# Masked softmax over 16 batches: stores in whole 16 KB packets, each held until the load five batches on has landed

## The chip, the core and the metric

The kernel runs on one core of a Trainium2 chip. The metric is the device time of the whole program in microseconds, as a median of several runs; the profile is a further execution, recorded by the hardware. The core's compute engines work beside 16 DMA engines, which move data between the chip's main memory (DRAM below) and the on-chip memory in which the tile `xt` lies.

## The reference: what is computed

The input `x` has 16 batches of 8 heads x 256 queries x 256 keys in float32: 2,048 rows of 256 numbers, 2 MB, for each batch. A vector `lengths` gives each batch the number of keys that count. Each row is a softmax over its first `length` keys, and zero behind them.

```python
for b in range(batch):
    length = lengths[b]
    masked = x[b, :, :, :length].copy()
    masked = masked - np.max(masked, axis=-1, keepdims=True)
    exp_masked = np.exp(masked)
    result[b, :, :, :length] = exp_masked / np.sum(exp_masked, axis=-1, keepdims=True)
```

The lengths of this draw are 188, 233, 229, 243, 195, 252, 165, 210, 222, 180, 209, 157, 159, 199, 214 and 248. The kernel does without the row's maximum.

## The kernel before: the parts that matter

A batch lies on 128 partitions, 16 rows of 256 numbers on each, so that one partition's share is 16 KB in one piece, in DRAM and in `xt` alike. `xt` has eight slots; batch b sits in slot b modulo 8 from its load to the end of its store.

**Loads.** The first four batches come whole, issued by the SP queue. Batches 4 to 15 are issued by GpSimd (POOL), which reads the length and loads only so many columns as are needed, in steps of eight (160, 168, ... 240, and 256 for the two longest): 16 short rows per partition rather than one long piece. Load n waits until load n-2 has landed and until store n-8, the last user of the slot, has landed.

```python
slots = 8
ahead = 4
...
for h in range(2):
    s = slice(h * half, (h + 1) * half)
    nc.sync.dma_start(out=xt[:, 0, s], in_=x_f[0, :, s]).then_inc(s_ld[h], 16)
for b in range(1, ahead):
    nc.sync.dma_start(out=xt[:, b], in_=x_f[b]).then_inc(s_ld[b + 1], 16)
...
nc.gpsimd.wait_ge(s_ld[ahead - 1], 16)
with nc.Fori(0, (batch - ahead) // 2, 1, engines=[POOL]) as q:
    for par in range(2):
        n = 2 * q + (ahead + par)
        v_len = length(POOL, word[0:1, bass.ds(2 * n, 1)])
        with nc.gpsimd.If(q >= 1):
            nc.gpsimd.wait_ge(s_sw[par], 16 * q)
            nc.gpsimd.wait_ge(s_st[par], 64 * q)
        pick(v_len, bass.ds(n, 1), bass.ds(n % slots, 1), par, widths + [seq_k])
...
# in pick, for the width w found:
nc.gpsimd.dma_start(out=xt[:, slot, :, :w], in_=x_n[:, n, :, :w]).then_inc(s_sw[par], 16)
```

`s_ld[3]` is the semaphore of batch 2. The semaphores `s_st` start at 64, set by GpSimd.

**Stores.** The SP queue stores a batch in parts. The first batch and batch 13 go whole, batches 1 to 7 as a half and two quarters, the rest in two halves. A half is 8 KB per partition, a quarter 4 KB. A part waits until its rows are divided (`s_out`); the first part of batch b also waits until store b-2 has landed.

```python
def parts(b):
    if b == 0:
        cuts = [0, nt]
    elif b < 8:
        cuts = [0, half, half + quarter, nt]
    elif b != batch - 3:
        cuts = [0, half, nt]
    else:
        cuts = [0, nt]
    return [slice(i, j) for i, j in zip(cuts, cuts[1:])]
...
nc.sync.wait_ge(s_exp, 3)
for b in range(batch):
    s_b = s_st[b % 2]
    for s in parts(b):
        nc.sync.wait_ge(s_out, 2 * b + (s.stop - 1) // half + 1)
        if b >= 2 and s.start == 0:
            nc.sync.wait_ge(s_b, 64 * (b // 2 + 1))
        nc.sync.dma_start(
            out=out_f[b, :, s, :], in_=xt[:, b % slots, s, :]
        ).then_inc(s_b, 16 * ((s.stop - s.start) // quarter))
```

**Compute.** Per batch VectorE (DVE) pushes the columns behind the length to a very negative number (`clip` in `mask`, one pass), ScalarE (ACT) takes 16 exponentials with their row sums, and DVE takes the reciprocals and multiplies, in two halves. Batch 4's mask waits for load 4, and so on.

Of the kernel before, what the change touches and what calls it, by code (L numbers as in the profile page):

```python
# [20 lines left out]
def kernel(  # L21
# [6 lines left out]
    nc = tc.nc  # L28
    P = nc.NUM_PARTITIONS

    batch, heads, seq_q, seq_k = x.shape
    rows = heads * seq_q
    assert rows % P == 0
    nt = rows // P
    half = nt // 2
    quarter = nt // 4
# [3 lines left out]

    slots = 8
    ahead = 4
    assert slots - ahead == 4 and batch % slots == 0

    widths = list(range(160, 248, 8))
    low = widths[0]
# [2 lines left out]

    def parts(b):  # L50


        if b == 0:
            cuts = [0, nt]
        elif b < 8:
            cuts = [0, half, half + quarter, nt]
        elif b != batch - 3:
            cuts = [0, half, nt]
        else:
            cuts = [0, nt]  # L60
        return [slice(i, j) for i, j in zip(cuts, cuts[1:])]

    pool = ctx.enter_context(tc.tile_pool(name="all", bufs=1))
# [17 lines left out]
    with tc.tile_critical(no_gpsimd_drain=True):  # L81
# [6 lines left out]
        s_sw = [sem("s_sw0"), sem("s_sw1")]  # L88
# [5 lines left out]
        s_exp = sem("s_exp")  # L94
# [15 lines left out]
        for b in range(1, ahead):  # L110
            nc.sync.dma_start(out=xt[:, b], in_=x_f[b]).then_inc(s_ld[b + 1], 16)  # L111

        nc.sync.wait_ge(s_exp, 3)
        for b in range(batch):
            s_b = s_st[b % 2]
            for s in parts(b):
                nc.sync.wait_ge(s_out, 2 * b + (s.stop - 1) // half + 1)
                if b >= 2 and s.start == 0:
# [4 lines that stand above are left out]
# [167 lines left out]
```

The softmax here doesn't subtract the row's maximum and nothing guards it: scores larger than these inputs give would overflow.

## Time and profile before

| | before |
|---|---|
| median of 3 runs | 156.5 us (156.17 to 156.55) |
| span of the profiled execution | 154.3 us |
| bytes moved by DMA | 62.08 MB: 28.51 MB read from DRAM, 33.55 MB written to it |
| mean rate over the span | 402 GB/s |
| DVE busy | 115.4 us (75%) |
| ACT busy | 105.2 us (68%) |
| POOL busy | 19.0 us (12%) |

In the page, a span is cut into 40 equal slices, and a digit is the busy share of a slice in tenths. A DMA queue (q0, q1) is a stream of transfers; q1 is that of SP, q0 that of GpSimd. A transfer is cut into packets, each of which one of the 16 DMA engines moves in one go. The records of the single packets in the trace give queue, start, duration and size of each; where the text speaks of packets' durations it means these. A window's line gives start and end, length, busy time of each engine with the number of its instructions, the granted clock, the DMA engines' mean busy share and the rate.

### The profile page before, as it was taken

The page shows a single profiled execution, that of the slowest core. Times are in us where ns is not written, and L with a number is a line of the kernel's source. Part 1 is how long each engine was busy: PE and PEld are TensorE (multiplying, and loading weights), DVE is VectorE, ACT ScalarE, POOL GpSimd, SP SyncE. Part 2 cuts the span into 40 slices and gives each one's busy share as a digit, 9 for nine tenths or more (in the row PEclk, how much of TensorE's full clock was granted, in tenths as well). Part 3 has the DMA queues.
Part 4 walks back from the last instruction along what each step waited for, and adds up shares of the span by engine and source line. Part 5 has one row for each costly group of instructions (what it writes and reads, how often), then busy time and mean ns, then how long its engine had stood idle before and what let it go on. Part 6 is the DMA issues. An engine that isn't in the chain of part 4 may idle for free.

```text
span 154.3 us, 1325 instructions
## 1 busy us (share of the span) xinstructions
PE 0.2 (0%) x1; PEld 0.1 (0%) x1; DVE 115.4 (75%) x84; ACT 105.2 (68%) x514; POOL 19.0 (12%) x25
## 2 busy tenths in 40 slices
PE   0000000000000000000000000000000000000000
PEld 0000000000000000000000000000000000000000
DVE  1339999952999696988969696969698692599500
ACT  3097799992592969779595959596877907988000
POOL 4910031000320200202011020202010000000000
DMA  4999999999999999999999999999999999999993
GB/s 117 427 450 420 437 365 409 400 408 452 407 406 390 415 404 417 412 413 415 405 419 413 414 412 405 416 416 420 417 416 423 418 431 435 418 444 418 423 431 130
DMA packets 10132, 62.08 MB, mean 402 GB/s; under 512 B 866, under 2 KB 962, under 8 KB 6290
## 3 DMA queue, kind: packets, MB, share of 16 engines
q1 hardware_dynamic: 6048, 41.95, 66.0%
q0 software_dynamic: 4080, 20.12, 32.2%
q14 instruction: 2, 0.02, 0.0%
q10 hardware_dynamic: 2, 0.00, 0.0%
HBM read 28.51 MB, written 33.55 MB: 402 GB/s over the span
## 4 chain that ended last, share of the span: by engine, by line
DMA 54%; DVE 25%; issue 7%; ACT 5%; ACTq 2%; SPq 1%; POOLq 1%; DVEq 0%
DMA xt<-in_x_dram 33%; DMA out_dram<-xt 21%; DVE xt L222 14%; DVE xt L195 9%; ACT xt L251 5%; ACTq L251 1%; DVE inv_sum L219 1%; SPq L109 1%; POOLq L99 0%; SPq L120 0%; SPq L111 0%; DVEq L212 0%; POOLq L130 0%; POOLq L135 0%; ACTq L246 0%
## 5 line engine op out<-in xcount | busy, mean ns | idle before, releaser
L251 ACT ACTIVATE xt<-xt x256 | 102.3, 401 | 35.2 <-DVE xt L195 35.2
L222 DVE TENSOR_TENSOR xt<-xt,inv_sum 128x2048 f32<-128x2048 f32 x32 | 73.4, 2292 | 1.1
L195 DVE SCALAR_TENSOR_TENSOR xt<-down,len_s,xt 128x2048 f32<-128x2048 f32 (+1 forms) x17 | 37.8, 2221 | 14.1 <-DMA xt<-in_x_dram 14.0
L251 ACT ACTIVATION_READ_ACCUMULATOR xt<-xt x256 | 47.9, 187 | 0.0
L130 POOL DMA_DIRECT2D xt<-in_x_dram x12 | 12.8, 1064 | 94.6 <-issue 48.7
L219 DVE RECIPROCAL inv_sum<-row_sum 128x8 f32<-128x8 f32 x32 | 6.3, 198 | 12.1 <-ACT xt L251 12.1
L149 POOL MEMSET xt<- 128x1536 f32 x4 | 5.3, 1386 | 1.1 <-DVE len_s L186 1.1
L243 ACT ACT_TABLE_LOAD x1 | 1.3, 1283 | 1.6 <-SPq L81 1.6
L178 DVE TENSOR_SCALAR down<-iota_i 128x256 f32<-128x256 int32 x1 | 0.3, 297 | 1.6 <-POOL iota_i L141 1.6
L183 DVE CAST len_b<-word 1x16 bf16<-1x16 int32 x1 | 0.2, 164 | 0.4 <-DMA word<-in_lengths_dram 0.4
L186 DVE TENSOR_SCALAR len_s<-len_f 128x16 f32<-128x16 f32 x1 | 0.2, 174 | 0.4 <-PE len_f L165 0.4
L141 POOL IOTA iota_i<- 128x256 int32 x1 | 0.3, 332 | 0.6 <-SPq L81 0.6
L146 POOL MEMSET seed<- 1x1 f32 x2 | 0.3, 162 | 0.0
L243 ACT ACTIVATE warm<-const-float32-0.0 128x1 f32<-128x1 f32 x1 | 0.2, 203 | 0.0
L144 POOL MEMSET ones<- 1x128 bf16 x1 | 0.2, 194 | 0.0
L165 PE MATMUL len_f<-len_b,ones 1*128 1x16 bf16 x1 | 0.2, 168 | 2.6 <-DVE len_b L183 2.6
L274 POOL MEMSET const-float32-0.0<- 128x1 f32 x1 | 0.1, 98 | 0.3 <-issue 0.3
L165 PEld LDWEIGHTS len_f<-len_b,ones 1*128 1x128 bf16 x1 | 0.1, 97 | 2.6 <-POOL ones L144 2.6
L274 POOL MEMSET const-float32-1.0<- 128x1 f32 x1 | 0.1, 98 | 0.0
L274 POOL MEMSET const-bfloat16-1.0<- 128x1 bf16 x1 | 0.1, 98 | 0.0
L274 POOL MEMSET const-uint8-127<- 128x1 uint8 x1 | 0.1, 98 | 0.0
L274 POOL BASE_LOAD x1 | 0.0, 17 | 0.1
## 6 DMA issues: line engine op xcount, KB each, us to landing
out_dram<-xt SPq DMA_DIRECT2D x21, 1024.0 KB
out_dram<-xt SPq DMA_DIRECT2D x14, 512.0 KB
xt<-in_x_dram SPq DMA_DIRECT2D x3, 2048.0 KB, 16.0
xt<-in_x_dram POOLq DMA_DIRECT2D x3, 1728.0 KB, 16.5
out_dram<-xt SPq DMA_DIRECT2D x2, 2048.0 KB
xt<-in_x_dram POOLq DMA_DIRECT2D x2, 2048.0 KB, 18.4
xt<-in_x_dram POOLq DMA_DIRECT2D x2, 1600.0 KB, 16.7
xt<-in_x_dram POOLq DMA_DIRECT2D x2, 1280.0 KB, 14.5
```

The source lines that it names most:

```text
L109: nc.sync.dma_start(out=xt[:, 0, s], in_=x_f[0, :, s]).then_inc(s_ld[h], 16)
L130: nc.gpsimd.dma_start(out=xt[:, slot, :, :w], in_=x_n[:, n, :, :w]).then_inc(s_sw[par], 16)
L141: nc.gpsimd.iota(iota_i, pattern=[[1, seq_k]], base=0, channel_multiplier=0).then_inc(s_iota, 1)
L146: nc.gpsimd.memset(seed[:, par : par + 1], 0.0).then_inc(s_st[par], 64)
L149: nc.gpsimd.memset(xt[:, b, :, low:], 0.0).then_inc(s_fill, 1)
L165: nc.tensor.matmul(len_f, lhsT=ones, rhs=len_b, start=True, stop=True).then_inc(s_lenf, 1)
L195: return nc.vector.scalar_tensor_tensor(out=t, in0=down[:, None, lo:hi].to_broadcast([P, s.stop - s.start, hi - lo]), scalar=len_s[:, b : ...
L219: step(nc.vector.reciprocal(out=inv_sum[:, b, s], in_=row_sum[:, b, s]))
L222: nc.vector.tensor_tensor(out=t, in0=t, in1=inv_sum[:, b, s, None].to_broadcast([P, half, seq_k]), op=ALU.mult,).then_inc(s_out, 1)
L243: nc.scalar.activation(out=warm, in_=nc.const_aps.tensor(0.0, (P, 1), F32), func=EXP)
L251: ins = nc.scalar.activation(out=e, in_=e, func=EXP, accum_out=sum_h[:, bass.ds(i, 1), j])
L274: nc = _bacc.Bacc("TRN2", target_bir_lowering=False, num_devices=1)
```

## The change

All stores go whole, with 16 KB per partition, but for the last batch, which goes in two halves. Before the store of batch b, SP now waits until load b+5 has landed, as long as there is such a load. The aim of the first is fewer and larger packets for the 33.55 MB that are stored. The aim of the second is that a store, with its large packets, does not take the DMA engines from loads that the compute will need: loads go first. The wait for the third exponential at the start falls away.

```diff
     slots = 8
     ahead = 4
-    assert slots - ahead == 4 and batch % slots == 0
+    lead = 5
+    assert slots - ahead == 4 and batch % slots == 0 and ahead <= lead < slots
...
     def parts(b):
 
-
-        if b == 0:
-            cuts = [0, nt]
-        elif b < 8:
-            cuts = [0, half, half + quarter, nt]
-        elif b != batch - 3:
-            cuts = [0, half, nt]
-        else:
-            cuts = [0, nt]
+        cuts = [0, nt] if b < batch - 1 else [0, half, nt]
         return [slice(i, j) for i, j in zip(cuts, cuts[1:])]
...
-        nc.sync.wait_ge(s_exp, 3)
+
         for b in range(batch):
             s_b = s_st[b % 2]
+            if b + lead < batch:
+                nc.sync.wait_ge(s_sw[(b + lead) % 2], 16 * ((b + lead - ahead) // 2 + 1))
             for s in parts(b):
                 nc.sync.wait_ge(s_out, 2 * b + (s.stop - 1) // half + 1)
```

Loads, compute and their order on POOL, DVE and ACT stay as they are. SP issues 17 stores in place of 37.

## The prediction, made before the result was known

> **What bounds the kernel now.** I looked first at the page's slices, since a kernel that moves 62 MB may be bound by nothing else:
>
> ```profile
> DMA  4999999999999999999999999999999999999993
> GB/s 117 427 450 420 437 365 409 400 408 452 407 406 390 415 404 417 412 413 415 405 419 413 414 412 405 416 416 420 417 416 423 418 431 435 418 444 418 423 431 130
> DMA packets 10132, 62.08 MB, mean 402 GB/s; under 512 B 866, under 2 KB 962, under 8 KB 6290
> ```
>
> The 16 DMA engines are busy in every slice but the first and the last. So the time is the sum of what the packets take; a change can win only by making packets cheaper, and loses whatever time it leaves the DMA engines empty. The queues say which packets:
>
> ```profile
> q1 hardware_dynamic: 6048, 41.95, 66.0%
> q0 software_dynamic: 4080, 20.12, 32.2%
> ```
>
> 66.0% + 32.2% of 154.3 us is 151.5 us of packet time, on engines that run from about 2.3 us to about 151.8 us (149.5 us). The sum exceeds the wall time by 1.3%, because neighbouring packets overlap a little. The windows show the same by stage, in the share column ahead of the rate:
>
> ```profile
> 20.00:24.00 4.00, 0.00 (x0) 0.00 (x0) 3.93 (x5) 4.00 (x22) 1.29 (x1) 1.00 0.99 356
> 44.00:92.00 48.00, 0.00 (x0) 0.00 (x0) 41.87 (x31) 35.51 (x175) 6.90 (x6) 1.00 1.02 410
> 100.00:116.00 16.00, 0.00 (x0) 0.00 (x0) 13.60 (x9) 12.98 (x64) 1.71 (x2) 1.00 1.02 418
> 134.00:150.00 16.00, 0.00 (x0) 0.00 (x0) 10.93 (x9) 7.41 (x38) 0.00 (x0) 1.00 1.01 428
> ```
>
> From 44 to 92 us short-row loads run beside 8 and 4 KB stores (410 GB/s), from 100 to 116 beside 8 KB stores alone (418), and from 134 only stores are left (428). The chain of waits agrees: DMA 54%, DVE 25%. DVE is busy 41.87 of the 48 us, so compute is not far behind, but stores trail it: before line 119, the wait for store b-2, SP spent 91.7 us.
>
> Last I looked at how a load starts, as the change makes stores depend on loads:
>
> ```profile
> 20.72 1.29 POOL L130 DMA_DIRECT2D xt<-in_x_dram  x1 [12.35 <-issue]
> 24.18 0.56 POOL L130 DMA_DIRECT2D xt<-in_x_dram  x1 [2.17 <-issue]
> 38.81 1.16 POOL L130 DMA_DIRECT2D xt<-in_x_dram  x1 [14.07 <-issue]
> 44.98 1.15 POOL L130 DMA_DIRECT2D xt<-in_x_dram  x1 [5.01 <-issue]
> ```
>
> These are loads 4 to 7. In the packet records, load 4's first packet starts at 26.23 us, 5.5 us after its issue, and load 6's at 43.86, 5.05 us after; load 6 had no load ahead of it any more, as load 5 was through at 42.93. So a short-row load takes about 5 us from issue to its first byte. Before it comes the wait itself: load 4 landed at 36.8 and load 6 was issued at 38.81; load 5 at 42.9 and load 7 at 44.98. That is 2.0 us from landing to issue. SP is quicker: its first load is issued at 1.13 us and its first packet starts at 2.17, 1.0 us later, and a store that waited for a landing was issued some 0.45 us after it (132.94 to 133.39).
>
> **What the Trainium skill says.** The page "DMA: Bandwidth & Descriptors", section "Queues, rings and completion order", says that a DMA engine takes turns between its queues packet by packet. The trace agrees: from 29 to 32 us, 8 KB stores (313 ns) and load 4's 4,800-byte packets (190 ns) hold 0.63 and 0.38 of the engines; 313:190 is 0.62:0.38. A 16 KB store packet (611 ns) beside a load packet of about 175 ns will therefore take 78%. The same page, section "Why small descriptors are slow (HBM only)", gives each packet a small fixed cost. Here, by median, 4 KB take 162 ns, 8 KB 313 and 16 KB 611: doubling costs 11 to 15 ns less than twice. The section "Anatomy of one DMA — SWDGE (gpsimd) path" calls descriptor generation "small, variable" and puts most of about 2 us of fixed cost into completion; here the 5 us ahead of the first byte are larger, so I take the trace.
>
> **Part 1, the packets removed.** Batches 1 to 7 go from 8+4+4 KB to 16 KB per partition: 313 + 2 x 162 - 611 = 26 ns, on 128 partitions over 16 engines 26 x 8 = 208 ns a batch, 1.46 us in all. Batches 8 to 12 and 14 go from 8+8 to 16 KB: (626 - 611) x 8 = 120 ns each, 0.72 us. Twenty transfers fewer save 20 x 16 completion packets of 9 ns, 0.18 us. Together 2.35 us, all on the path, as nothing but packets is. Some 0.23 us come on top, by which store 0's packets were slow (641 ns on average) while it met the end of load 3. Sum: -2.6 us.
>
> **Part 2, the wait at the start.** In the kernel before, store 0 (issued at 19.75) fills the engines from the end of load 3 until load 4's first byte. Afterwards store 0 waits for load 5. Load 3's bytes end near 23 us; load 4 is still issued at 20.72, since its wait (batch 2) is unchanged, so its bytes start near 26.0, allowing for a start without a 16 KB packet in the way. By 26.2 the old kernel had moved 9.72 MB; the new one will have only the four loads' 8.39 MB. The difference, 1.33 MB at 0.42 MB/us, is 3.1 us.
>
> **Part 3, a second gap.** From 26.0, load 4 alone takes 4.1 us (1.64 MB by its packets' durations) and load 5 4.9 us (2.1 MB in 16 KB packets): they land near 30.4 and 35.3. Load 6 is issued at 30.4 + 2.0 and can move nothing before 37.4. Store 0 starts at 35.3 + 0.45 + 1.0 = 36.8. From 35.0 to 36.8 the engines are empty: 1.8 us.
>
> **Part 4, the steady state.** Load 8 waits for store 0, so now store b waits for load b+5 and load b+5 for store b-3. I walked through it: when load n ends, store n-5 needs 0.4 + 0.45 + 1.0 = 1.9 us to its first byte, in which load n+1 moves alone (some 10 packets per engine); then store n-5's 8 packets per engine alternate with 8 of load n+1, 8 x (611 + 175) = 6.3 us; then load n+1 has, for 216 columns, 7 of 25 packets left, 1.2 us. Turn: 9.4 us. Load n+2, issued 2.0 us after load n landed, is ready after 7.1 to 7.5 us: just in time, also with the shortest rows (160 columns, 19 packets, 8.3 us). So no gap, by a margin of under 1 us for loads 12 and 13. Behind load 15 nothing is left to cover store 10's start, but load 15 has 16 KB packets and shares evenly with store 9, which ends about when store 10 starts: 0.2 us.
>
> The alternation with large packets has fewer changes of queue, and overlap falls from 1.02 in the mixed windows towards the 1.01 of a lone queue: about 0.5% of 90 us, 0.45 us. At the end both kernels run stores back to back; compute is done earlier there than before and does not matter.
>
> **Sum.** 156.5 - 2.6 + 3.1 + 1.8 + 0.2 + 0.45 = 159.45. A count from 26.0 onwards gives a little less: 127.8 us of packets at 1.2% overlap is 126.3, plus 2.0 of gaps, to 154.3, against 151.8 before: +2.5, so 159.0. I take 159.1.
>
> **Rivals.** First, that the gap at the start is not there: if the 5 us of load 4 are caused by store traffic or by the busy DVE (3.93 of 4 us from 20 to 24), an idle DMA may start it sooner. Against it: load 6 shows the same 5 us in other traffic, and DVE will be as busy there. Then parts 2 and 3 shrink to about 2 us together and the time is 156 to 156.5. Second, that compute gains because load 4 lands at 30.4 rather than 36.8; DVE waited 14.0 us for loads. It does, but the DMA engines, which set the end, get nothing from it: no change. If instead the stores were held back by compute, it would give 153; the 91.7 us before line 119 speak against it. Third, that short-row loads alone on the engines run slower than mixed; no stretch of the trace shows it. At 10% slower, on some 25 us, it would add 2.5 us, 161.5. Fourth, that the margin of part 4 fails for several loads, each then adding up to 1 us: 160 to 163.
>
> **Range and chances.** 2% off is 153.4 and 159.6. The centre lies just inside the upper one. For lower values speaks the first rival, for higher ones the third and fourth; to get below 153.4 both gaps would have to be missing. I take 156.4 to 161.8, with 0.06 for faster, 0.52 for the same and 0.42 for slower.
>
> **What would show it.** The DMA slices should show two dents, near 23 to 26 and 35 to 37 us, and none later. 16 KB stores should take 611 ns in the packet records, queue q1 some 2.3 us of 16 engines less. SP's waits for DMA should name loads in place of stores. DVE should wait for many loads, for short times. Engines full near 24 us would refute part 2; dents once a batch, part 4; a lower rate in full slices, part 1.

## The result: 161.17 us after 156.33 us

The changed kernel takes 161.17 us (median of 4 runs, 160.27 to 161.47), the kernel before 156.33 us beside it. The ratio is 1.030, with a 95% interval of 1.0254 to 1.0345: slower. The profiled execution has a span of 159.8 us against 154.3, 5.5 us more.

The page of the changed kernel, slices and queues (packets, megabytes, share of 16 engines' span):

```profile
DMA  4999989989999999999999999999999999999993
GB/s 121 441 422 443 422 289 344 439 253 338 425 391 426 374 422 398 384 409 368 430 385 432 383 412 356 409 400 367 440 414 451 410 426 435 418 447 410 447 404 150
DMA packets 7252, 62.08 MB, mean 388 GB/s; under 512 B 546, under 2 KB 642, under 8 KB 4178
...
q1 hardware_dynamic: 3168, 41.94, 62.5%
q0 software_dynamic: 4080, 20.12, 34.8%
```

The same bytes go in 2,880 packets fewer, and the engines are marked busy nearly throughout: only the slices at 20 to 24 and 32 to 36 us are an 8. Yet the rate sways between 253 and 451 GB/s in the slices between the first and the last. Read in microseconds, queue q1 (first loads and all stores) falls from 66.0% of 154.3 = 101.8 us to 62.5% of 159.8 = 99.9 us: the cheaper store packets are there. Queue q0, GpSimd's loads, rises from 32.2% of 154.3 = 49.7 us to 34.8% of 159.8 = 55.6 us, for the same 4,080 packets and the same bytes. That is the loss. The windows of the changed kernel (start and end, length, busy us of PE, PEld, DVE, ACT and POOL, clock, DMA share, GB/s) show when:

```profile
20.00:24.00 4.00, 0.00 (x0) 0.00 (x0) 3.93 (x5) 4.00 (x21) 1.86 (x2) 1.00 0.81 289
24.00:28.00 4.00, 0.00 (x0) 0.00 (x0) 4.00 (x2) 4.00 (x21) 0.00 (x0) 1.00 0.99 344
34.00:38.00 4.00, 0.00 (x0) 0.00 (x0) 3.97 (x4) 4.00 (x21) 1.15 (x1) 1.00 0.92 271
44.00:92.00 48.00, 0.00 (x0) 0.00 (x0) 40.66 (x30) 37.23 (x183) 5.76 (x5) 1.00 1.01 400
108.00:112.00 4.00, 0.00 (x0) 0.00 (x0) 4.00 (x2) 2.60 (x14) 0.56 (x1) 1.00 1.03 365
134.00:150.00 16.00, 0.00 (x0) 0.00 (x0) 5.02 (x5) 3.03 (x16) 0.00 (x0) 1.00 1.01 430
```

From 24 to 28, 34 to 38 and 108 to 112 us the packet records hold load packets alone, no store. The engines are busy (0.92 to 1.03) and slow (271 to 365 GB/s). In the store-only end the rate is 430 against 428 before. SP's own waits, and the start of the loads on POOL:

```profile
SPq L115 <- DMA xt<-in_x_dram: 85.9, 11, 16.2
SPq L114 <- DMA out_dram<-xt: 37.5, 10, 5.0
```

```profile
20.94 1.30 POOL L125 DMA_DIRECT2D xt<-in_x_dram  x1 [12.55 <-issue]
23.23 0.56 POOL L125 DMA_DIRECT2D xt<-in_x_dram  x1 [0.99 <-issue]
31.56 1.16 POOL L125 DMA_DIRECT2D xt<-in_x_dram  x1 [7.76 <-issue]
36.51 1.15 POOL L125 DMA_DIRECT2D xt<-in_x_dram  x1 [3.80 <-issue]
```

Stores now wait 85.9 us for loads. Load 4 is issued at 20.94 and its first packet starts at 23.05, load 6 at 31.56 and 33.44: 1.9 to 2.1 us, where it was 5 us before. DVE was as busy in both kernels (3.93 of the 4 us from 20 to 24), so most of those 5 us had been the store traffic in the way.

The packet records give the median of a full packet, by whether any store packet overlaps it:

| row of the load | rows a packet | beside 8 or more store packets (before) | alone (after) | alone, ns a row |
|---|---|---|---|---|
| 640 B (11, 12) | 7 | 179 ns | 201 ns | 28.7 |
| 672 B (6) | 7 | 194 ns | 261 ns | 37.3 |
| 736 B (9) | 6 | 174 ns | 229 ns | 38.2 |
| 800 B (4) | 6 | 191 ns | 229 ns | 38.2 |
| 864 B (10, 14) | 5 | 171 ns | 192 ns | 38.4 |
| 896 B (8) | 5 | 176 ns | 192 ns | 38.4 |
| 1,024 B (5), one 16 KB packet | 16 | 611 ns | 615 ns | 38.4 |

Beside stores, a row costs nearly by its bytes. Alone, a row of 672 to 896 bytes takes as long as a whole one of 1,024, so the bytes saved by such short loads buy no time. Some loads reach this price only after a while: load 4's packets take 185 ns until 25.5 us and 229 from 26, and load 13 (800 B too), alone for 50 packets near 108 us, rises from 185 to 229 ns. Of all load packet time after, 32.4 us has no store packet beside it; before, none had.

### The profile page after: what moved, and what is told of

It reads as the page before. It is cut to its first block, busy times and chain, and to the rows that moved or that the text cites. A ratio compares the mean times of both kernels' runs of the same rounds, so it can differ in the third digit from the quotient of the medians.

```text
span 159.8 us, 1306 instructions
## 1 busy us (share of the span) xinstructions
PE 0.2 (0%) x1; PEld 0.1 (0%) x1; DVE 115.5 (72%) x84; ACT 105.2 (66%) x514; POOL 19.0 (12%) x25
## 3 DMA queue, kind: packets, MB, share of 16 engines
q1 hardware_dynamic: 3168, 41.94, 62.5%
q0 software_dynamic: 4080, 20.12, 34.8%
HBM read 28.51 MB, written 33.55 MB: 388 GB/s over the span
## 4 chain that ended last, share of the span: by engine, by line
DMA 61%; ACT 9%; issue 8%; DVE 5%; POOLq 2%; ACTq 1%; SPq 1%; DVEq 0%; POOL 0%
DMA xt<-in_x_dram 61%; ACT xt L246 9%; DVE xt L190 3%; DVE xt L217 2%; ACTq L246 1%; POOLq L130 1%; POOLq L125 1%; POOLq L92 1%; SPq L102 1%; POOL xt L125 0%; DVEq L92 0%; DVE inv_sum L214 0%; SPq L104 0%; ACTq L241 0%; POOLq L152 0%
## 5 line engine op out<-in xcount | busy, mean ns | idle before, releaser
L246 ACT ACTIVATE xt<-xt x256 | 102.6, 406 | 30.2 <-DVE xt L190 30.2
L246 ACT ACTIVATION_READ_ACCUMULATOR xt<-xt x256 | 49.0, 191 | 0.0
```

The lines of the kernel that those rows point to most:

```text
L246: ins = nc.scalar.activation(out=e, in_=e, func=EXP, accum_out=sum_h[:, bass.ds(i, 1), j])
```

## The experiments

The theories. **A**: short-row loads take longer per packet when they have the engines to themselves, and the change makes that happen. **B**: the harm is the large store packet, which holds most of the engines. **C**: the wait itself costs, by empty engines and turns. The table gives the whole account: medians of 4 runs (12 and 11 for the last two); from the profiled execution the span, the packet time of both queues by the packet records without the completion packets, and the time in which engines were empty (the missing share in all tenths of a microsecond, between 3 us and the last store, that are under 95% full). One run each of lead6 (171.78) and align_new (162.32) lies over 1.5% above the fastest of its kernel; without them the medians are 169.21 and 160.67.

| run | median us | ratio to before, 95% | span | q0 | q1 | empty |
|---|---|---|---|---|---|---|
| before | 156.33 | | 154.3 | 49.5 | 101.5 | 0.4 |
| after | 161.17 | 1.030 (1.0254 to 1.0345) | 159.8 | 55.5 | 99.6 | 1.5 |
| whole_no_gate | 164.03 | 1.051 (1.0477 to 1.0551) | 162.3 | 53.7 | 100.5 | 5.3 |
| old_parts_gate | 161.42 | 1.033 (1.0278 to 1.0379) | 159.9 | 54.3 | 101.4 | 1.2 |
| wide_old | 166.24 | 1.065 (1.0615 to 1.0676) | 164.6 | 58.8 | 100.9 | 1.7 |
| wide_new | 164.22 | 1.052 (1.0493 to 1.0550) | 162.4 | 59.8 | 98.7 | 0.3 |
| w64_old | 161.48 | 1.034 (1.0311 to 1.0361) | 159.7 | 55.2 | 100.8 | 0.7 |
| w64_new | 164.60 | 1.054 (1.0498 to 1.0590) | 162.8 | 59.3 | 99.2 | 1.0 |
| lead4 | 159.82 | 1.023 (1.0202 to 1.0256) | 158.0 | 54.2 | 99.7 | 1.0 |
| lead6 | 170.13 | 1.087 (1.0789 to 1.0959) | 167.6 | 60.6 | 98.8 | 4.9 |
| align_new | 161.08 | 1.035 (1.0302 to 1.0389) | 158.3 | 54.1 | 99.5 | 1.5 |
| w64_align_new | 164.77 | 1.056 (1.0518 to 1.0594) | 163.1 | 58.9 | 99.6 | 1.2 |
| align_old | 156.61 | 1.003 (1.0013 to 1.0048) | 155.0 | 49.5 | 101.9 | 0.8 |
| early_old | 156.78 | 1.004 (1.0029 to 1.0056) | 155.1 | 49.8 | 101.7 | 0.8 |

For the change: +6.0 (q0) - 1.9 (q1) + 1.1 (empty) = +5.2 us, of 5.5. The same sum gives the span's difference to before within 0.7 us in every other row.

The 6.0 us of q0 have two parts. 1.9 us are what 86 full load packets of over 300 ns took beyond the median of their load (185 to 261 ns); 1.8 us of it lies at the start of loads 4, 6 and 13. The kernel before had 3 such packets (for 16 KB packets counted from 700 ns). The other 4.1 us or so are the steadily slower rows of the table above. The experiments below are about those; what makes single packets slow, none of them isolates.

### Each half of the change by itself

`whole_no_gate`, against the changed kernel:

```diff
-            if b + lead < batch:
-                nc.sync.wait_ge(s_sw[(b + lead) % 2], 16 * ((b + lead - ahead) // 2 + 1))
```

> Whole stores, without the wait for the load five batches on. Theory A (short-row loads take longer per packet when they have the DMA engines to themselves, and the wait for the load drives loads and stores apart): without that wait both queues stay filled, load packets stay near 171 ns for 4,320 bytes, and the cheaper store packets show: 154 to 156.5 us. Theory B (the large store packets are the harm, since they hold 78% of the engines and loads then run alone): 159 to 162 us, as the change itself.

It took 164.03 us, more than the change and more than theory B's 159 to 162. So whole stores alone do harm, as theory B had it, and the wait takes part of that back. The page, the waits and one line of DVE's timeline of this run:

```profile
DMA  4999999999989999999999999999999999990995
GB/s 127 446 432 428 428 299 419 425 424 441 412 338 269 369 421 426 402 423 407 391 412 404 420 395 410 371 422 389 404 417 381 441 421 436 424 388 4 388 420 226
```

```profile
DVE xt L188 <- DMA xt<-in_x_dram: 23.3, 7, 10.7
```

```profile
142.57 2.35 DVE L188 SCALAR_TENSOR_TENSOR xt<-down,len_s,xt 128x2048 f32<-128x2048 f32 x1 [4.35 <-DMA xt<-in_x_dram]
```

Load 4 needs from 25.96 to 42.37 us beside the large packets: 16.4 us, and 10.6 in the kernel before. DVE waits for it, no store is ready, and loads 5 and 6 have the engines to themselves: whole-row load 5 still passes at 431 GB/s in the packet records, short-row load 6 brings the slices from 44.6 to 52.7 us down to 338 and 269. In the end load 15 lands at 141.9 instead of 132.1 us. DVE waits for it before it divides batch 14, so the stores of the last two batches come late; all others are done by then, and the engines stand empty for 4.7 us: the slice with a 0. The account is q0 +4.2, q1 -1.0, empty +4.9. Theory B is right on the cause here, but part of its cost runs through theory A: starved loads end up alone.

`old_parts_gate`, the changed kernel with the old cuts:

```diff
-        cuts = [0, nt] if b < batch - 1 else [0, half, nt]
+        (the four cases of the kernel before)
```

> The old parts (halves and quarters), with the wait for the load five batches on. Theory A: loads still run alone at the start (loads 4 and 5, and 6 until store 0 starts) and for part of each turn, though less, since a store in small packets leaves more to the load beside it: 158 to 162 us, with 4,320-byte load packets well over 171 ns on average. Theory B: 156 to 157.5 us.

161.42 us: theory A's figure; B had 156 to 157.5. With the old small packets, the wait alone costs 5.3 us, and q0 has +4.8 in its account. The two halves do not add, 7.9 and 5.3 us, each against the kernel before beside it, and 4.8 for both: the wait cures the starving that whole stores cause, and brings its own loss.

### Without short rows

`wide_old` and `wide_new` load all 256 columns in both kernels:

```diff
-                pick(v_len, bass.ds(n, 1), bass.ds(n % slots, 1), par, widths + [seq_k])
+                pick(v_len, bass.ds(n, 1), bass.ds(n % slots, 1), par, [seq_k])
```

> The kernel before, but every load from batch 4 on takes all 256 columns, so that it moves 16 KB pieces (25.17 MB in place of 20.12 MB; the saving of bytes is left out). It is the base for the next run. Both theories: packet time grows by 12 x 4.89 - 49.6 = 9.1 us, so some 165 us.

> The changed kernel with all 256 columns loaded. There are no short rows. Theory A: nothing is left of the 6 us by which load packets grew; the store packets' 2.3 us count, the gaps of about 1 to 2 us remain, so it is from 2 us faster to 1 us slower than the kernel before with wide loads. Theory C (the wait itself costs: gaps and turns in which only one kind of transfer is under way, whatever the packets): some 5 us slower than the kernel before with wide loads.

166.24 us before the change and 164.22 after it; the runs do not overlap (166.05 to 166.43, 164.06 to 164.42). Without short rows the change is 2.0 us *faster*. Theory C falls for this wait: the same waits and turns cost nothing here. Stores keep their gain (q1 -2.2 us), load packets grow by only 1.0 us, and that is 48 slow packets (over 700 ns) in load 6, most of them from 34.5 to 37.5 us; the medians of all twelve loads stay at 611 to 614 ns, alone or not. The window of wide_new in which loads run alone as 16 KB pieces, for the 344 GB/s of the changed kernel at the same place:

```profile
23.00:27.00 4.00, 0.00 (x0) 0.00 (x0) 3.97 (x4) 4.00 (x21) 0.00 (x0) 1.00 1.01 430
```

### How far apart loads and stores are driven

`lead4` and `lead6` change the one number of the wait:

```diff
-    lead = 5
+    lead = 4      # lead6: 6
```

> The changed kernel with the wait for the load four batches on, so that one more transfer can be under way. Theory A: loads run alone for less of the time, load packet time falls from 55.6 us towards 52, and it takes 157 to 160 us. If the share of 78% that large store packets take is what matters most (theory B), it goes the way of the kernel without the wait: 161 to 164 us.

> The changed kernel with the wait for the load six batches on: one transfer fewer can be under way. Theory A: loads run alone longer, and empty stretches appear as each store waits for a landing, 163 to 168 us. Theory B: the longer loads go first the better, 158 to 161 us.

159.82, 161.17 and 170.13 us for 4, 5 and 6. Theory A had the order. lead4 gains as expected, though its q0 falls only to 54.2 us, not 52. lead6 is worse than expected: q0 reaches 60.6 us, with 53.4 us of packets beside no store, and 4.9 us are empty, seen as the 8s of its page. Of q0's 11.1 us over the kernel before, 6.8 are the excess of 340 slow packets, so here the slow packets cost more than the steady price of short rows does (the other 4.3 us); in lead4 39 slow packets cost 0.8 us. The page of lead6:

```profile
DMA  4999989899999999989999889998999999999993
GB/s 141 442 430 430 434 274 385 362 262 321 372 435 374 342 318 400 426 313 355 337 445 430 298 265 305 431 418 279 406 375 418 438 438 434 438 430 426 426 413 151
```

### Why a row alone takes longer

The sharper form of A came from the row table: alone, 640 bytes take as long as 768 would, 672 to 896 as 1,024. I first took it for a rounding of the row's length, so that 768-byte rows would pass in 28.7 ns.

`w64_new` and `w64_old`, with 192 and 256 columns only:

```diff
-    widths = list(range(160, 248, 8))
+    widths = [192]
```

> The changed kernel with only two widths to choose from, 192 and 256 columns, so that loads 4 to 15 read 23.07 MB in place of 20.12. Theory A in its sharper form (alone on the engines, a row of 672 to 896 bytes takes as long as one of 1,024, 38.2 ns, and one of 640 as long as one of 768): four loads at 128 rows an engine x 28.7 ns and eight at 38.2 ns are 53.8 us of packets against 55.6 in the changed kernel, so in spite of 2.95 MB more it is no slower: 158.5 to 161.5 us. Theory D (alone, short rows merely lose a fixed share or a fixed time to each packet): the bytes count, and 2.95 MB at 0.42 MB/us add 7 us: 167 to 169 us.

> The kernel before with the same two widths. Its loads run beside stores, where a row's time goes by its bytes. Both theories: 2.95 MB more add some 6 to 7 us, 162 to 163.5 us.

The base took 161.48 us, a little under what was expected. The changed kernel took 164.60: neither the 158.5 to 161.5 of that form nor the 167 to 169 of theory D. The packet tells why: six rows of 768 bytes alone took 232 ns, 38.7 ns a row, like 1,024 and not like 768. (This is the median over loads 6, 9 and 12. Loads 9 and 12 rise to 232 to 234 ns, while load 6 starts at 178 and reaches only 222.) So 640 bytes cost three units of about 9.55 ns (38.2 / 4) and 672 and 768 four. That fits a row that starts 128 bytes off a multiple of 256 and pays for each 256-byte stretch it touches: 128 + 640 fills three, 128 + 672 reaches into a fourth, 128 + 896 fills it. In the built program, `xt` starts at byte 16,512 of each partition, 128 off a multiple of 256. The Trainium skill, page "DMA: Bandwidth & Descriptors", section "How a descriptor splits into AXI transactions", describes such splitting at 256-byte boundaries, for what is read; here the side written is the one that was off.

`align_new`, `w64_align_new` and `align_old` move `xt` by 128 bytes in the changed kernel, in w64_new and in the kernel before:

```diff
+    gap = pool.tile([P, 32], F32, name="gap")
     xt = pool.tile([P, slots, nt, seq_k], F32, name="xt")
```

> The changed kernel with an unused tile of 128 bytes per partition ahead of xt, so that xt starts at a multiple of 256 bytes in each partition (byte 16,640) and not 128 bytes off one (16,512). Theory A256 (alone on the engines, a row costs 9.55 ns for each 256-byte stretch of the on-chip memory that it touches): rows of 672 and 736 bytes touch three stretches in place of four, 28.7 ns a row in place of 38; rows of 640 stay at 28.7 and rows of 800 to 896 at 38. Loads 6 and 9 alone get about 1.5 us cheaper: 159 to 160.5 us. Theory R (the rounding has nothing to do with where xt starts): packets as before, 160.3 to 161.5 us.

> The changed kernel with the two widths 192 and 256, and with the 128 bytes ahead of xt. Theory A256: a row of 768 bytes then touches three stretches, and a packet of six such rows alone takes 172 ns in place of 232: 161.5 to 163.5 us against 164.6. Theory R: the packet stays at 232 ns and the time at 164.3 to 165.6 us.

> The kernel before with the 128 bytes ahead of xt. Both theories: its loads run beside stores throughout, where a row's time goes by its bytes, so load packets stay where they are and the time is the same within 0.5%. If packets got cheaper here too, 4,704 bytes at 185 ns and less, it would be 155 to 156 us, better than both kernels.

Median of a full packet alone on the engines, as before and after the move:

| row | 672 B | 736 B | 768 B | 640 B | 800 B | 864 B | 896 B |
|---|---|---|---|---|---|---|---|
| xt 128 B off | 261 ns | 229 ns | 232 ns | 201 ns | 229 ns | 192 ns | 192 ns |
| xt at a multiple of 256 | 188 ns | 181 ns | 191 ns | 201 ns | 229 ns | 192 ns | 192 ns |

Just the three kinds of row change that should, and the four others do not. The place of the tile in a partition is a cause. They come to 26.9, 30.2 and 31.8 ns a row, where 28.7 was expected for each: they rise with the bytes, and lie within 4% of what the same rows take beside stores (194, 174 and 184 ns a packet), so the step is not the whole of it. The times, however, missed what was expected of them: 161.08 us, with runs from 159.92 to 162.32, and 164.77. In the profile of align_new q0 falls by 1.4 us, as expected, but that execution was the fastest of the four. Whether the gain is there in the median, these runs do not say. In w64_align_new q0 falls by only 0.4 us; its slow packets cost 3.8 us, and 2.7 in w64_new. In the kernel before, where no load is alone, load 6's packets fall a little (194 to 187 ns), those of the other loads stay, and the time gains nothing: 1.003 (1.0013 to 1.0048), if anything a loss.

`early_old`, the kernel before with load 4 issued while batches 2 and 3 are still being loaded:

```diff
-        nc.gpsimd.wait_ge(s_ld[ahead - 1], 16)
+        nc.gpsimd.wait_ge(s_ld[1], 16)
```

> The kernel before, in which GpSimd waits for batch 0 in place of batch 2 before it issues load 4, so that load 4 runs beside the whole loads of batches 2 and 3 and no store. Theory A-queue (any second queue that takes turns hides the rounding of a row): load 4's packets of 4,800 bytes take 191 ns. Theory A-store (only stores in the other direction hide it): 229 ns. The time is 155 to 158 us by both, as batches 2 and 3 land later and load 4 sooner.

Load 4's packets took 185 ns (191 beside the whole loads), by the letter the answer "any queue". Its neighbours say otherwise. From 18 to 23.5 us, beside load 4, the whole loads' 16 KB packets have a median of 654 ns in place of 611, beside load packets of 191: a pair takes 845 ns, as much as the two alone (611 + 229 = 840), at 402 GB/s by the packet records. The price was paid; it stood in the other packet. From 27 to 32 us the 16 KB packets are those of store 0: 611 ns, beside load packets of 185, so 796 ns a pair and 429 GB/s. Two windows of this run, the rates counted by where packets start:

```profile
18.00:23.00 5.00, 0.00 (x0) 0.00 (x0) 3.08 (x3) 5.00 (x26) 0.00 (x0) 1.00 1.04 413
26.00:32.00 6.00, 0.00 (x0) 0.00 (x0) 5.55 (x4) 4.85 (x26) 0.00 (x0) 1.00 1.01 431
```

So in this run stores hid the price, and turns with another load did not. Why is not shown. A possible reason is that a store does not write to the on-chip memory, so that the writing side gets time to catch up. The first packets of load 4 in the changed kernel, 185 ns until 25.5 us and 229 from 26, would fit it, as if a buffer had filled, but that side's working was not measured by itself. The time of the whole kernel did not gain, 1.004.

No version beat the kernel before.

## Why the prediction was right in its range, and where its steps failed

The 161.17 us lie in the range of 156.4 to 161.8, 2.1 us above the centre. "Slower", at 0.42, came true, though "same" had the larger chance, 0.52. The terms of its sum fared unequally, and that the number came so close is partly luck: 3.8 us of the 4.9 us of empty engines did not come, and a cost that stood only among the rivals came in their place.

**What bounds the kernel**: right. DMA packet time and empty engines account for the whole difference in every run.

**Part 1**, -2.6 us for cheaper store packets: right in kind, -1.9 us measured. The medians are as said, 611 ns, but the mean of the 16 KB packets on q1 is 618. The sign that was named against it, a lower rate in full slices, did come (338 GB/s from 36 to 40 us, in a slice marked 9), but from the loads.

**Part 2**, 3.1 us by which the new kernel would lag at the start: the gap is 0.7 us (22.3 to 24.3). The step that failed is "so its bytes start near 26.0". The 5 us from issue to first byte had been read from two loads that both met stores; without stores it is 1.9 to 2.1 us. The first rival said so. It named 156 to 156.5 us as the consequence, which did not come, because the loads that started early then ran slowly: load 4's packets cost 1.1 us more than before, load 6's 1.6.

**Part 3**, a second gap of 1.8 us: 0.4 us (32.9 to 34.8), for the same reason: load 6 began at 33.44, not 37.4. Store 0, in turn, was not quick. Issued at 35.09, its first packet starts at 38.41. Over the ten stores 0 to 9 this takes 1.4 to 4.5 us, where "0.45 + 1.0" had been taken from an empty queue at the start of the program. So a turn can leave a load alone for longer than the 1.9 us of part 4.

Where the time would go was seen better than how. By 26.2 us the changed kernel is 0.39 MB behind (9.33 against 9.72), by 40 us 1.53 MB (13.98 against 15.51); at the prediction's 0.42 MB/us that is an estimated 0.9 and 3.6 us, where parts 2 and 3 add up to 4.9. Only 1.1 us of it is empty engines; the rest is load packets that take longer.

**Part 4**, no gaps in the steady state: right, the slices there are all 9s. But the load beside a store did not go as the walk had it. Load n+2, issued into store traffic, came late again (load 8: issued at 47.88, first packet at 52.54, though load 7 was through on the first of the engines at 49.35), and the store had the engines nearly to itself at its end. Loads and stores took turns rather than ran side by side.

**The third rival**, short rows alone run slower, was the answer, put at "10% slower, on some 25 us, it would add 2.5 us". It measured 6.0 us: 32.4 us of load packets entirely without a store, 10.9 more with fewer than eight store packets beside them, 9% to 35% per packet in the medians of the table, by where the row ends, and in it the 1.9 us of slow packets, of which the rival had no word. With the measured terms the sum is 156.5 - 1.9 + 6.0 + 1.1, or 161.7: the account closes, but only with sizes known afterwards. DVE, which was to wait for many loads, waited for three, 7.8 us in all. The kernel before has no stretch of short rows alone, so its trace could not give the size; what it could show is that rows of 640 to 896 bytes had never been seen without stores.

## What to carry to other kernels

A transfer's packet time is not a property of the transfer: here the same packets cost 12% more in all once loads and stores no longer overlapped, with the engines marked busy all the while. Before adding a wait that puts one kind of transfer ahead of another, look at whether the trace shows that kind alone, and at what rate; and watch GB/s, not only the busy share. A latency from issue to first byte should be taken from the traffic in which it will be needed.

## What was not expected of the hardware

- Alone on the engines, and with a tile that starts 128 bytes off a multiple of 256, a row took 28.7 ns for 640 bytes and 37 to 39 for 672 to 896, which fits about 9.55 ns for each 256-byte stretch of the on-chip memory that it touches. Moving the tile by 128 bytes brought 672, 736 and 768 bytes to 26.9, 30.2 and 31.8 ns, which no longer fits one price a stretch. Beside stores the step does not show, and the place only in the 672-byte row (194 to 187 ns a packet).
- From issue to first byte, GpSimd's loads took 1.9 to 2.1 us with no store under way, and about 5 us beside stores; SP's stores took 1.4 to 4.5 us beside loads.
- The first packets of a load on emptied engines were slow: in the changed kernel, load 6's first packets, at 33.5 to 34 us, took a median of 798 ns. Load 6 also went on at 264 to 267 ns from 36 to 38.5 us, above the 229 ns of other alone loads but with seven rows in a packet, so at the same 38 ns a row. Why the first ones are slow was not tried. In wide_new most such packets came after load 6 had run for 2 us at 611 ns, so being first is not the whole of it.
